# Attention scores on two row halves of the tensor array, two units at a time, with gelu given out in two steps

## The chip, the cores and the metric

The kernel runs on one core of one Trainium2 chip. The metric is the device time of one execution in microseconds (us); the kernel before has three timed runs, 1193.89, 1192.25 and 1193.23 us, and their median is 1193.23 us. The profile is of one further execution, which took 1194.63 us from end to end, of which 1192.8 us are the span that the trace covers.

A core has five engines with a queue of instructions each: TensorE (PE, matrix products; its weight loads are shown apart as PEld), VectorE (DVE), ScalarE (ACT), GpSimd (POOL), and SyncE (SP), which here only starts DMA transfers. Each works its queue in order, and an instruction that has to wait holds up all that stands behind it. SBUF is the memory that the engines work from, PSUM the eight banks that TensorE writes to.

## The reference

Two transformer layers over 512 tokens of width 1024, and 256 context tokens. Layer 0 mixes tokens with a gated product (gelu of an input projection, one half normalised and mixed by a spatial matrix, times the other half) and, beside it, with attention in 8 heads of width 64: a token on the 8 x 64 grid attends to a window of 8 rows and 16 columns, with a position bias, and to all context tokens, under one softmax. Layer 1 is a convolution module. Both have a squared-ReLU MLP. The part that is changed:

```python
    s_loc = jnp.einsum('brqhd,brkwhd->bhrqkw', qg, k_band).astype(jnp.float32) * scale + bias[None]
    s_loc = jnp.where(col_mask[:, None, :], s_loc, NEG)
    s_ctx = jnp.einsum('brqhd,bchd->bhrqc', qg, k_ctx).astype(jnp.float32) * scale
    s = jnp.concatenate([s_loc.reshape(bsz, nh, rows_n, GRID_W, n_loc), s_ctx], axis=-1)
    p = jax.nn.softmax(s, axis=-1).astype(v.dtype)
    out = (jnp.einsum('bhrqkw,brkwhd->brqhd', p_loc, v_band)
           + jnp.einsum('bhrqc,bchd->brqhd', p_ctx, v_ctx))
```

and `jax.nn.gelu(z)` in the gated product. Every layer's six modulation vectors are products of a vector with a matrix, `sc_c @ w_mod[l] + b_mod[l]`.

## The kernel before, in words

A large product is done in three passes of TensorE (`mm3`, L88 to L90): each operand is split into a rounded part "hi" and a rest "lo", and hi x hi, hi x lo and lo x hi are added in one PSUM bank. The split is a CAST (L93) and a subtraction (L94). Weights come as 1 MB tiles (`raw`, L120) in two buffers, are cut into quarters (`W.pieces`, cast on ACT, subtraction on POOL or DVE), and are used from `whi`/`wlo`.

The attention stage lies between about 82 and 236 us of the span. It goes through 16 **units**, 4 pairs of heads (p) times 4 tiles of 128 queries (j). A unit is worked in these steps:

- S, the scores (`scores`, L88 to L90): for each head of the pair 128 queries against 256 windowed keys and 256 context keys into one bank of 128 x 512. Queries, keys and context keys of a pair hold one head on partitions 0 to 63 and the other on 64 to 127. So that a product over all 128 partitions counts one head only, `evac_qk` writes the queries twice, each time with the other head's half multiplied by zero (L542, and L93, L94 for each copy). That gives 12 matmuls of 256 columns for a unit.
- R, on DVE (L771), adds bias and mask and takes the row's minimum of the negated sum; the exponential follows on ACT (L775).
- T, the turn (`turn`, L788): 8 transposes on PE of the unit's probabilities, copied to SBUF by ACT (`pt`, L790). In the last unit of a pair a RECIPROCAL of the row sums stands ahead of it on DVE (L783).
- W, the product with v (`weigh`, L804): 16 matmuls that use 64 columns of the array. After a pair's fourth unit, 8 small matmuls spread the reciprocals (L812, "RECIPbc" below), ACT copies them (`rs`, L816), and DVE scales the pair's output with them (`yb`, L818).

The order is written by hand in the loop over units. Between these steps stands other work: **fills** (`more(1)`, the next step of the generator `filling()`: values of the later pairs, queries and keys of pairs 2 and 3, then the gate with its gelu), mostly 6 matmuls of 512 columns or 12 of 256; and **gemvs** (`work`, L505), the modulation products of later layers, each one DVE pass over 1024 columns of half a 1 MB tile `graw`. There is one buffer for `graw` in this stage, and the load of the next tile (SP, L498) is issued when the second gemv of the tile before is done. 24 gemvs, 12 tiles, fall into this stage, two to a unit. SP's queue also holds the loads of `raw` (each waits until POOL has cut the buffer that it replaces) and of the bias rows (L658). The 12 biases of a pair (`head_bias`, L670) are made on DVE in units j = 2 and j = 3 of the pair ahead.

After the loop the last two row blocks of the gated product are made (`together`, L210 to L213), with a gelu each, and the output projection of the layer begins.

## Time and profile before

| | |
|---|---|
| three timed runs | 1193.89, 1192.25, 1193.23 us, median 1193.23 us |
| profiled execution | 1194.63 us, span 1192.8 us, mean granted TensorE clock 0.993 |
| busy in the span | PE 1162.5 us (97%), DVE 730.5 us (61%), ACT 475.5 us (40%), POOL 173.7 us (15%) |
| attention stage, first scores to first product of `together` | 84.71 to 235.50 us |
| spread of the pairs' reciprocals on PE (L812) | 125.33, 160.45, 199.23 and 231.68 us |

A row of the timeline gives the start in us, the duration, the engine (SPq is SP's queue of DMA issues), the line, the operation, out<-in, the tile's shape on the array (rows\*columns, PE only), the operand's shape and how many are drawn together; in brackets stands how long the engine was idle before and what released it. A row of the stretches gives the stretch, its length, and busy time and count for PE, PEld, DVE, ACT and POOL, then the granted TensorE clock, the busy share of the DMA engines and GB/s. PE's instructions are pipelined, so the time that one takes is read from start to start.

### The profile page before, as it was taken

To read this page: it belongs to the slowest core of one execution; us is meant where nothing else is said; L and a number is where in the kernel's file an instruction comes from. 1 tells how busy PE (TensorE), PEld (TensorE's weight loads), DVE (VectorE), ACT (ScalarE), POOL (GpSimd) and SP (SyncE) were. 2 spreads that over 40 slices of the span, in tenths; PEclk is the share of its full clock that TensorE was granted. 3 is DMA by queue.
4 is the path that set the end of the run, shared out by engine and by line. 5 is a ranking of instruction groups with operands and counts; after the bars stand their busy time and mean duration, and the time that the engine had idled before them with its cause. 6 is when DMAs were issued, how large, how long until landed. Compare 5 with 4: busy or idle time off the path is not lost.

```text
span 1192.8 us, 16638 instructions
## 1 busy us (share of the span) xinstructions
PE 1162.5 (97%) x6662; PEld 968.6 (81%) x6662; DVE 730.5 (61%) x1248; ACT 475.5 (40%) x942; POOL 173.7 (15%) x166
## 2 busy tenths in 40 slices
PE   6999999999999999999999999999999999999997
PEld 2688889779988888888889856688988888888887
DVE  4675777557775666675757778577743443443445
ACT  4463545454632332341425523465642232332423
POOL 1231225263200000000003310044200000000001
PEclk9999999999999999999999999999999999999999
DMA  9624543134155554554543344404132222332322
GB/s 363 233 81 146 186 169 109 70 141 141 60 226 209 182 205 180 207 206 153 208 141 111 108 122 133 130 2 142 36 106 107 84 98 101 105 106 72 106 71 71
DMA packets 30605, 161.91 MB, mean 136 GB/s; under 512 B 4224, under 2 KB 7808, under 8 KB 12608
## 3 DMA queue, kind: packets, MB, share of 16 engines
q1 hardware_dynamic: 30528, 160.85, 38.5%
q8 instruction: 52, 0.85, 0.3%
q14 instruction: 25, 0.20, 0.0%
HBM read 152.52 MB, written 2.10 MB: 130 GB/s over the span
## 4 chain that ended last, share of the span: by engine, by line
PE 80%; DVE 6%; DMA 3%; ACT 2%; issue 1%; POOL 1%; DVEq 0%; SPq 0%; ACTq 0%; POOLq 0%
PE ps L88 21%; PE ps L89 21%; PE ps L90 21%; PE ps L1160 3%; PE ps L213 3%; PE ps L210 3%; PE ps L211 3%; DMA graw<-in_wmB_dram 2%; DVE graw L505 1%; DMA raw<-in_w_ff_dram 1%; PE ps L695 1%; PE ps L804 1%; PE ps L696 1%; PE ps L697 1%; ACT s L775 1%
## 5 line engine op out<-in xcount | busy, mean ns | idle before, releaser
L93 ACT CAST whi<-raw 128x512 fp32r<-128x512 f32 x340 | 191.4, 616 | 198.2 <-PE ps L90 152.6
L88 PE MATMUL ps<-hhi,whi 128*128 128x512 f32 x640 | 253.1, 395 | 1.4 <-ACT hhi L341 1.4
L89 PE MATMUL ps<-hhi,wlo 128*128 128x512 f32 x640 | 250.3, 391 | 1.0 <-DVE wlo L94 1.0
L90 PE MATMUL ps<-hlo,whi 128*128 128x512 f32 x640 | 249.8, 390 | 0.7 <-DVE hlo L349 0.7
L94 DVE TENSOR_TENSOR wlo<-raw,whi 128x512 fp32r<-128x512 f32 x280 | 193.7, 728 | 34.8 <-ACT whi L93 34.0
L90 PE MATMUL ps<-hid,whi 128*128 128x512 f32 (+1 forms) x520 | 196.3, 378 | 0.0
L89 PE MATMUL ps<-hid,wlo 128*128 128x512 f32 (+1 forms) x520 | 196.3, 378 | 0.0
L88 PE MATMUL ps<-hid,whi 128*128 128x512 f32 (+1 forms) x520 | 196.3, 378 | 0.0
L910 DVE SCALAR_TENSOR_TENSOR x<-ps,mod,x 128x512 f32<-128x512 f32 (+1 forms) x94 | 62.7, 668 | 156.5 <-PE ps L90 151.3
L94 POOL TENSOR_TENSOR wlo<-raw,whi 128x512 fp32r<-128x512 f32 x60 | 86.1, 1449 | 478.1 <-ACT whi L93 477.6
L88 PEld LDWEIGHTS ps<-hhi,whi 128*128 128x128 f32 x640 | 120.7, 189 | 33.1 <-issue 6.1
L90 PEld LDWEIGHTS ps<-hlo,whi 128*128 128x128 f32 x640 | 120.6, 188 | 26.6 <-DVE hlo L349 1.0
L89 PEld LDWEIGHTS ps<-hhi,wlo 128*128 128x128 f32 x640 | 120.8, 189 | 25.0 <-DVE wlo L94 1.3
L505 DVE CUSTOM_DVE_ANT_0 graw<-graw,cB,vec 128x1024 f32<-128x1024 f32 x80 | 103.4, 1302 | 18.1 <-DMA graw<-in_wmB_dram 18.1
L88 PEld LDWEIGHTS ps<-hid,whi 128*128 128x128 f32 x520 | 97.8, 188 | 18.2
L90 PEld LDWEIGHTS ps<-hid,whi 128*128 128x128 f32 x520 | 97.8, 188 | 18.2
L89 PEld LDWEIGHTS ps<-hid,wlo 128*128 128x128 f32 x520 | 97.8, 188 | 18.0
L1036 DVE TENSOR_TENSOR z<-z 128x512 f32<-128x512 f32 (+1 forms) x72 | 46.3, 649 | 94.4 <-ACT z L1034 94.4
L1034 ACT ACTIVATE z<-ps 128x512 f32<-128x512 f32 (+1 forms) x72 | 38.9, 550 | 139.4 <-PE ps L90 136.8
L1040 DVE TENSOR_TENSOR hid<-z,hid 128x512 fp32r<-128x512 f32 (+1 forms) x72 | 45.7, 641 | 43.3 <-ACT hid L1038 43.3
L1038 ACT CAST hid<-z 128x512 fp32r<-128x512 f32 (+1 forms) x72 | 40.6, 572 | 51.7 <-DVE z L1036 51.7
L1390 POOL TENSOR_TENSOR o<-o,rstd 128x256 f32<-128x256 f32 x2 | 1.9, 949 | 322.2 <-DVE rstd L322 322.2
(261 smaller groups left out, 1757.2 us busy)
## 6 DMA issues: line engine op xcount, KB each, us to landing
raw<-in_w_ff_dram SPq DMA_DIRECT2D x64, 1024.0 KB
graw<-in_wmB_dram SPq DMA_DIRECT2D x40, 1024.0 KB
raw<-in_w_pw_dram SPq DMA_DIRECT2D x12, 1024.0 KB
raw<-in_w_in_dram SPq DMA_DIRECT2D x10, 1024.0 KB
wmA<-in_wmA_dram SPq DMA_DIRECT2D x7, 1024.0 KB
y<-ypad SPq DMA_DIRECT2D x90, 67.5 KB
raw<-in_w_out_dram SPq DMA_DIRECT2D x4, 1024.0 KB
x<-in_xT_dram SPq DMA_DIRECT2D x8, 256.0 KB
```

The source lines that it names most:

```text
L88: pe.matmul(ps, w[0], a[0], start=first, stop=False)
L89: pe.matmul(ps, w[1], a[0], start=False, stop=False)
L90: pe.matmul(ps, w[0], a[1], start=False, stop=last)
L93: (e or act.copy)(hi, src)
L94: (el or dve).tensor_tensor(lo, src, hi.bitcast(F32), op=ALU.subtract)
L210: pe.matmul(ps, w[0][:, k, c : c + P], a[0], start=n == 0, stop=False)
L505: dve.tensor_tensor_reduce(out=wv, in0=wv, in1=cB, scale=1.0, scalar=vcol(V_BMOD, l * 48 + q * 8 + j % 8), op0=ALU.mult, op1=ALU.add, accu ...
L910: dve.scalar_tensor_tensor(x[:, m, t0:t1], ps, gate[:, m : m + 1], x[:, m, t0:t1], op0=ALU.mult, op1=ALU.add)
L1034: act.activation(z, ps, AF.Relu)
L1036: dve.tensor_tensor(z, z, z, op=ALU.mult)
L1038: act.copy(hi, z)
L1040: dve.tensor_tensor(lo, z, hi.bitcast(F32), op=ALU.subtract)
```

## The change

Lines of the changed program are named by the changed program's numbers; R is L799, the exponential L803, the scores L786, T L816, W L832, RECIPbc L840, yb L846, the reciprocal L811 in it.

- **Scores.** Queries are written once for both heads of a pair, scaled by 0.125 (one ACTIVATE, one CAST, one subtraction where there were two each). Context keys go into the same tile behind the pair's keys. A product takes one head's 64 partitions, on rows 0 to 63 or 64 to 127 of the array, against 512 columns (256 window keys and 256 context keys in one access pattern). A unit has 6 matmuls of 512 columns, the two heads' in turn, where it had 12 of 256 columns.
- **Two units per turn of the loop.** Both units' scores stand together, behind them the products with v of the two units before, then R of the first unit, a fill, R of the second, two or three fills, T of the first, biases of two heads (j = 2), a fill, four gemvs, T of the second, two or three fills. `scores` gives R back as a function. Loads of bias rows are issued two at a time.
- **Gelu in two steps.** `gelu2` yields ahead of its Tanh; the second half is given out at the next fill (`stage`), so another's first half can stand between. The last two gelus start together.
- **Buffers.** The `mblk` pool has 8 tiles where it had 14, `sg` and every second unit's `pt` come from other pools, and the keys have a pool of their own. `graw` keeps its one buffer.

```diff
@@ -532,22 +532,21 @@
     def tok(t):
         return t.rearrange("p (r b c) -> p r b c", b=8, r=8)
 
-    q_s, k_s, kc_s, v_s = {}, {}, {}, {}
+    q_s, k_s, v_s = {}, {}, {}
 
     def evac_qk(m, ps, t0, t1):
         kind, p_ = m
         if kind == "q":
-            for e in range(2):
-                t = slot(s="qt")
-                act.activation(perm(t), tok(ps), AF.Copy, scale=kon[:, C_HEAD + e : C_HEAD + e + 1])
-                pr = (aslot(F32R, "qh"), aslot(F32R, "ql"))
-                split(pr[0], pr[1], t, dve.tensor_copy)
-                q_s[2 * p_ + e] = pr
+            t = slot(s="qt")
+            act.activation(perm(t), tok(ps), AF.Copy, scale=0.125)
+            pr = (aslot(F32R, "qh"), aslot(F32R, "ql"))
+            split(pr[0], pr[1], t, dve.tensor_copy)
+            q_s[p_] = pr
         else:
             t = slot(s="kt")
             act.copy(perm(t), tok(ps))
-            pr = (mslot(F32R, "kh"), mslot(F32R, "kl"))
-            split(pr[0], pr[1], t, dve.tensor_copy)
+            pr = tuple(mp.tile([P, T + TC], F32R, tag="keys", name=nm(n), bufs=4) for n in ("kh", "kl"))
+            split(pr[0][:, :T], pr[1][:, :T], t, dve.tensor_copy)
             k_s[p_] = pr
 
     def first_v():
@@ -582,10 +581,9 @@
             mm3(ps, (w[0][:, k, c : c + P], w[1][:, k, c : c + P]), hc[k], k == 0, k == KC - 1)
             if k == 3:
                 yield
-        t = mslot(F32R, "kc")
-        act.copy(t[:, :TC], ps)
-        dve.tensor_tensor(t[:, TC:], ps, t[:, :TC].bitcast(F32), op=ALU.subtract)
-        kc_s[p_] = (t[:, :TC], t[:, TC:])
+        hi, lo = (t[:, T:] for t in k_s[p_])
+        act.copy(hi, ps)
+        dve.tensor_tensor(lo, ps, hi.bitcast(F32), op=ALU.subtract)
         yield
 
     def turn_v(m, t):
@@ -683,8 +681,21 @@
         t = slot(cols=n, s="gelu")
         act.activation(t, ps, AF.Square, scale=math.sqrt(0.044715))
         dve.scalar_tensor_tensor(t, t, 1.0, ps, op0=ALU.add, op1=ALU.mult)
+        yield
         act.activation(t, t, AF.Tanh, scale=math.sqrt(2.0 / math.pi))
         dve.scalar_tensor_tensor(dst, t, 1.0, ps, op0=ALU.add, op1=ALU.mult)
+
+    staged = deque()
+
+    def stage(n=None):
+
+        for g in list(staged)[:n]:
+            if next(g, 1):
+                staged.remove(g)
+
+    def begin(g):
+        next(g)
+        staged.append(g)
 
     def gate(i):
         w = W.use()
@@ -700,13 +711,18 @@
             if i == 0:
                 gn[n] = mslot(s="gn")
             gt = gn[n][:, i * 256 : (i + 1) * 256]
-            gelu2(gt, ps, 256)
-            for e in range(2):
-                bs = small(6, "bs")
-                dve.bn_stats(bs, gt[:, e * P : (e + 1) * P])
-                dve.bn_aggr(gmv[:, n, 2 * i + e, :], bs)
+
+            def rest(gt=gt, ps=ps, n=n):
+                yield from gelu2(gt, ps, 256)
+                for e in range(2):
+                    bs = small(6, "bs")
+                    dve.bn_stats(bs, gt[:, e * P : (e + 1) * P])
+                    dve.bn_aggr(gmv[:, n, 2 * i + e, :], bs)
+
+            begin(rest())
             yield
         W.free()
+        stage()
 
     def gate_norm(i):
         sd = small(8, "gsd")
@@ -749,19 +768,28 @@
     sm, pts, po, yb, tot = {}, {}, {}, {}, {}
 
     def scores(u):
+
         p_, j = units[u]
         b0 = KSTART[j] // 8
         if j == 0:
             tot[p_] = mp.tile([P, 8], F32, tag="tot", name=nm("tot"), bufs=2)
-        kk = tuple(k_s[p_][i][:, b0 * 64 : b0 * 64 + 256] for i in range(2))
-        pss = []
-        for e in range(2):
-            hd = 2 * p_ + e
-            ps = bank()
-            qh = tuple(q_s[hd][i][:, j * P : (j + 1) * P] for i in range(2))
-            mm3(ps[:, :256], qh, kk, True, True)
-            mm3(ps[:, 256:], qh, kc_s[p_], True, True)
-            pss.append(ps)
+
+        def keys(i, e):
+
+            t = k_s[p_][i][64 * e : 64 * e + 64, :]
+            return bass.AP(t.tensor, t.offset + b0 * 64, [t.ap[0], [T - b0 * 64, 2], [1, 256]])
+
+
+        pss = [bank() for e in range(2)]
+        for n, (a, b) in enumerate(((0, 0), (0, 1), (1, 0))):
+            for e in range(2):
+                pe.matmul(pss[e].rearrange("p (a b) -> p a b", b=256),
+                          q_s[p_][a][64 * e : 64 * e + 64, j * P : (j + 1) * P], keys(b, e),
+                          start=n == 0, stop=n == 2)
+        return lambda: soften(u, pss)
+
+    def soften(u, pss):
+        p_, j = units[u]
         res = []
         for e in range(2):
             hd = 2 * p_ + e
@@ -786,7 +814,7 @@
             pt = bank()
             for i in range(4):
                 pe.transpose(pt[:, i * P : (i + 1) * P], s[:, i * P : (i + 1) * P], ident)
-            t = mp.tile([P, 512], F32, tag="pt", name=nm("pt"), bufs=2)
+            t = blk(s="pt") if u % 2 else mp.tile([P, 512], F32, tag="pt", name=nm("pt"), bufs=2)
             act.copy(t, pt)
             pts[u].append(t)
         del sm[u]
@@ -848,34 +876,38 @@
 
     def more(n):
         for _ in range(n):
+            begun = len(staged)
             if next(fill, 1) is None:
                 nfill[0] += 1
+            stage(begun)
             W.pieces(1, pool)
 
+
     NU = len(units)
-    for u in range(NU):
+    for u in range(0, NU, 2):
         p_, j = units[u]
-        if p_ < 3 and j in (0, 1):
-            rows[2 * p_ + 2 + j] = load_bias(2 * p_ + 2 + j)
-        scores(u)
-        more(1)
+        if p_ < 3 and j == 0:
+            for e in range(2):
+                rows[2 * p_ + 2 + e] = load_bias(2 * p_ + 2 + e)
+        left = [scores(u), scores(u + 1)]
         if u >= 2:
             weigh(u - 2)
+            weigh(u - 1)
+        left[0]()
         more(1)
-        p_, j = units[u]
-        if u >= 1:
-            turn(u - 1)
-        if p_ < 3 and j in (2, 3):
-            head_bias(2 * p_ + j, rows.pop(2 * p_ + j))
+        left[1]()
+        more(2 if u < 8 else 3)
+        turn(u)
+        if p_ < 3 and j == 2:
+            for e in range(2):
+                head_bias(2 * p_ + 2 + e, rows.pop(2 * p_ + 2 + e))
         more(1)
-        work(1 if u in (10, 11) else 2 if u < 13 else 0)
-        if u in (7, 11):
+        work(4 if u < 12 else 0)
+        turn(u + 1)
+        more(2 if u < 8 else 3)
+        if u in (6, 10):
             later.popleft()()
-        if u >= 8:
-            more(1)
     weigh(NU - 2)
-    turn(NU - 1)
-    more(2)
     weigh(NU - 1)
     more(100)
 
@@ -892,12 +924,13 @@
     ev = iter(evs)
     next(ev)()
     W.pieces(1, pool)
+    next(ev)()
+    stage()
+    W.pieces(1, pool)
     operand(2)
     W.pieces(1, pool)
-    next(ev)()
-    W.pieces(1, pool)
     operand(3)
-    
+
     mix.close()
     ma.close()
     xp = ctx.enter_context(tc.tile_pool(name="stream", bufs=1))
```

On DVE, in the first units, the gemvs stand so before (units 0 to 3; `graw` with another number is another 1 MB tile):

```order
L771 ISA st_828 128x1
L505 ISA graw_803,mod_414<-graw_803,cB,vec 128x1024
L505 ISA mod_414 128x1
L505 ISA graw_803,mod_414<-graw_803,cB,vec 128x1024
L505 ISA mod_414 128x1
L771 ISA s_877,st_878<-ps_863,biases 128x512
L771 ISA st_878 128x1
L771 ISA s_881,st_882<-ps_870,biases 128x512
L771 ISA st_882 128x1
L505 ISA graw_858,mod_414<-graw_858,cB,vec 128x1024
```

and so with the change:

```order
L799 ISA s_835,st_836<-ps_807,biases 128x512
L799 ISA st_836 128x1
L505 ISA graw_789,mod_414<-graw_789,cB,vec 128x1024
L505 ISA mod_414 128x1
L505 ISA graw_789,mod_414<-graw_789,cB,vec 128x1024
L505 ISA mod_414 128x1
L505 ISA graw_879,mod_414<-graw_879,cB,vec 128x1024
L505 ISA mod_414 128x1
L505 ISA graw_879,mod_414<-graw_879,cB,vec 128x1024
L505 ISA mod_414 128x1
L799 ISA s_945,st_946<-ps_912,biases 128x512
```

The rows of two tiles now follow one another with no R between them, and the second tile's load can be issued only after the first tile's second row.

At the end of the first pair of heads, DVE before (the reciprocal, then a whole unit's gemvs and R, then the scaling `yb`):

```order
L783 RECIPROCAL tot_808<-tot_808 128x8
L505 ISA graw_1097,mod_415<-graw_1097,cB,vec 128x1024
L505 ISA mod_415 128x1
L505 ISA graw_1097,mod_415<-graw_1097,cB,vec 128x1024
L505 ISA mod_415 128x1
L771 ISA s_1196,st_1197<-ps_1182,biases 128x512
L771 ISA st_1197 128x1
L771 ISA s_1200,st_1201<-ps_1189,biases 128x512
L771 ISA st_1201 128x1
```

and with the change:

```order
L505 ISA graw_1029,mod_414<-graw_1029,cB,vec 128x1024
L505 ISA mod_414 128x1
L505 ISA graw_1029,mod_414<-graw_1029,cB,vec 128x1024
L505 ISA mod_414 128x1
L811 RECIPROCAL tot_797<-tot_797 128x8
L846 TENSOR_TENSOR yb_1126<-ps_928,rs_1124 128x512
L799 ISA s_1128,st_1129<-ps_1083,biases 128x512
L799 ISA st_1129 128x1
```

The reciprocal stands behind the run of four gemvs, and `yb` directly behind the reciprocal, ahead of the next R.

On PE, one unit's scores before, all on the full array:

```order
L88 MATMUL ps_1006<-kh_554,qh_542 128x256
L89 MATMUL ps_1006<-kh_554,ql_543 128x256
L90 MATMUL ps_1006<-kl_555,qh_542 128x256
L88 MATMUL ps_1006<-kc_678,qh_542 128x256
L89 MATMUL ps_1006<-kc_678,ql_543 128x256
L90 MATMUL ps_1006<-kc_678,qh_542 128x256
L88 MATMUL ps_1013<-kh_554,qh_548 128x256
```

and with the change, the two heads' banks in turn, with the products with v (L832) behind two units' scores:

```order
L786 MATMUL ps_920<-kh_548,qh_542 128x512
L786 MATMUL ps_921<-kh_548,qh_542 128x512
L786 MATMUL ps_920<-kl_549,qh_542 128x512
L786 MATMUL ps_921<-kl_549,qh_542 128x512
L786 MATMUL ps_920<-kh_548,ql_543 128x512
L786 MATMUL ps_921<-kh_548,ql_543 128x512
L832 MATMUL ps_928<-pt_860,vtok_765 64x128
```

Six rows for a unit stand where twelve stood, each twice as wide.

## The prediction

> **What bounds the kernel now.** I read the page first, then the stretches of the attention stage, then the timeline of one unit, and last the queues of DVE and SP between two units.

> ```profile
> PE 1162.5 (97%) x6662; PEld 968.6 (81%) x6662; DVE 730.5 (61%) x1248; ACT 475.5 (40%) x942; POOL 173.7 (15%) x166
> PE 80%; DVE 6%; DMA 3%; ACT 2%; issue 1%; POOL 1%; DVEq 0%; SPq 0%; ACTq 0%; POOLq 0%
> 100.00:120.00 20.00, 20.00 (x167) 17.71 (x166) 13.15 (x35) 6.11 (x16) 0.00 (x0) 1.00 0.36 125
> ```

> PE is the bound, over the span (97%) and in the stage (20.00 of 20.00 us), while DVE has a third of its time free (13.15 of 20). So PE work taken out here is time won, as long as DVE's free third stays usable. One unit on PE:

> ```profile
> 113.81 0.28 PE L88 MATMUL ps<-kh,qh 128*128 128x256 f32 x1
> 115.25 0.40 PE L88 MATMUL ps<-hhi,whi 128*128 128x512 f32 x1
> 115.48 0.40 PE L89 MATMUL ps<-hhi,wlo 128*128 128x512 f32 x1
> 116.73 0.66 PE L804 MATMUL ps<-pt,vtok 128*64 128x128 f32 x8
> 117.75 0.50 PE L88 MATMUL ps<-hhi,whi 128*128 128x512 f32 x1
> 118.09 0.40 PE L89 MATMUL ps<-hhi,wlo 128*128 128x512 f32 x1
> 119.25 1.03 PE L788 MATMUL ps<-kon,s 128*128 128x128 f32 x8
> 120.04 0.48 PE L88 MATMUL ps<-hhi,whi 128*128 128x512 f32 x1
> ```

> S takes 115.25 - 113.81 = 1.44, W 1.02, T 0.79; 512 columns take 0.23 from start to start, a fill of six 1.41. Going into W costs about 0.09 and the first product behind it 0.34 instead of 0.23: 0.2 to 0.24 for each change between full array and halves. Now DVE and SP in units 2 and 3:

> ```profile
> 93.98 0.33 SPq L120 DMA_DIRECT2D raw<-in_w_in_dram  x1
> 94.41 0.38 SPq L498 DMA_DIRECT2D graw<-in_wmB_dram  x1
> 101.53 1.29 DVE L505 CUSTOM_DVE_ANT_0 graw<-graw,cB,vec 128x1024 f32<-128x1024 f32 x1 [7.40 <-DMA graw<-in_wmB_dram]
> 102.74 1.28 DVE L505 CUSTOM_DVE_ANT_0 graw<-graw,cB,vec 128x1024 f32<-128x1024 f32 x1
> 103.95 0.69 DVE L771 CUSTOM_DVE_ANT_1 s<-ps,biases 128x512 f32<-128x512 f32 x1
> 104.06 0.33 SPq L498 DMA_DIRECT2D graw<-in_wmB_dram  x1
> 104.56 0.69 DVE L771 CUSTOM_DVE_ANT_1 s<-ps,biases 128x512 f32<-128x512 f32 x1
> 108.94 1.28 DVE L505 CUSTOM_DVE_ANT_0 graw<-graw,cB,vec 128x1024 f32<-128x1024 f32 x1 [2.48 <-DMA graw<-in_wmB_dram]
> ```

> A gemv is 1.21, R 0.61 a head. From a load's issue to its first gemv pass 4.9 us (104.06 to 108.94), or 7.1 with a raw load just ahead of it in SP's queue (94.41 to 101.53). DVE stands still for part of that, but PE has its queue full and doesn't notice.

> **What the change takes from PE.** Six matmuls of 512 columns in pairs of row halves: if two halves overlap fully, 3 x 0.23 = 0.70 a unit, saving 0.74; if not at all, 6 x 0.23 = 1.39, saving 0.05. Nearest row, two other shapes of product:

> ```profile
> 14.19 1.07 PE L392 MATMUL ps<-graw,sc 128*32 128x512 f32 x8 [0.32 <-DMA graw<-in_wmA_dram]
> 18.85 1.02 PE L381 MATMUL ps<-dgc,ones 128*128 128x512 f32 x2
> ```

> Eight quarter-array products of 512 columns took as long as two whole ones, so parts of the array do run side by side; I take 0.70. Sixteen units: 11.8. Scores next to W share its mode change: about 1.0 for all. [...] No run here shows row halves.) Nearly all of the 12.8 is cover that DVE uses up, as follows.

> **What it adds: a load's wait inside DVE's queue.** Two units' four gemvs now stand in a row with one `graw` buffer. The second tile's load is issued behind the first tile's second gemv, so the run is 2.42 + 4.9 + 2.42 = 9.8 us, 5 of them idle, and behind it wait the next R (then the exponential and T on PE) and, at the end of a pair, the reciprocal for which PE's RECIPbc waits. PE can't run ahead: it works its queue in order. The marks for the sum are the four RECIPbc:

> ```profile
> 125.33 1.04 PE L812 MATMUL ps<-kon,tot 128*64 128x128 f32 x16
> 160.45 1.09 PE L812 MATMUL ps<-kon,tot 128*64 128x128 f32 x16 [0.68 <-DVE tot L783]
> 199.23 1.04 PE L812 MATMUL ps<-kon,tot 128*64 128x128 f32 x16
> 231.68 1.04 PE L812 MATMUL ps<-kon,tot 128*64 128x128 f32 x16
> 233.39 0.69 DVE L818 TENSOR_TENSOR yb<-ps,rs 128x512 f32<-128x512 f32 x1 [7.20 <-ACT rs L816]
> 235.50 0.39 PE L210 MATMUL ps<-hhi,whi 128*128 128x512 f32 x1
> ```

> The fills between marks differ, so each stretch of before is corrected by the fills that change sides. (Plus: gained.)

> A, start to first mark. Before it was 125.33 with four more fills ahead, equal to 119.7. After:

> ```profile
> 84.71 0.58 PE L88 MATMUL ps<-kh,qh 128*128 128x256 f32 x1 [2.90 <-DVE kc L587]
> 84.00:86.00 2.00, 1.29 (x6) 1.29 (x7) 0.99 (x4) 0.00 (x0) 0.00 (x0) 0.65 0.92 377
> 86.00:88.00 2.00, 2.00 (x10) 1.90 (x10) 1.02 (x3) 0.76 (x2) 0.00 (x0) 0.50 0.58 219
> 89.28 1.28 DVE L505 CUSTOM_DVE_ANT_0 graw<-graw,cB,vec 128x1024 f32<-128x1024 f32 x1 [0.90 <-DMA graw<-in_wmB_dram]
> 105.17 1.30 DVE L670 TENSOR_TENSOR biases<-rows,kon 128x128 f32<-128x128 f32 x6
> ```

> Two pairs' queries are split here, so two casts and subtractions less (2.2) and the copies ahead of them on ACT shorten DVE's queue at the start by about 3, which removes the 2.90 stall and most of what the clock cost behind it (0.65 and 0.50 in the next two stretches, about 1.5). PE then starts at 81.8. But this is given back at once: tile 0 lands at 89.28 as before, since its load stands in SP's queue behind a raw load that waits for POOL, whose work there is unchanged. From there: 2.42, the second load 6 (between 4.9 and 7.1, a raw load is near), 2.42, four R 2.46, twelve biases 2.46, 2.42, 4.9, 2.42: the reciprocal at about 115. PE alone would be there near 111.5, which is 81.8 plus six S 4.2, four T and four W 7.6, twelve fills 16.9 and mode changes 1.0. **+4.6** (3.5 to 5.7).

> B, first to second mark. Before 35.1, corrected by a fill 33.7. After, on DVE:

> ```profile
> 129.93 1.24 ACT L542 ACTIVATE qt<-ps,kon 128x512 f32<-128x512 f32 x2
> 130.63 0.43 DVE L93 CAST qh<-qt 128x512 fp32r<-128x512 f32 x1 [1.55 <-ACT qt L542]
> 131.09 0.69 DVE L94 TENSOR_TENSOR ql<-qt,qh 128x512 fp32r<-128x512 f32 x1
> ```

> RECIPbc, copy and yb 2.35 (231.68 to 234.0), R 2.46, then the queries' split, whose PE product ends only four fills and a T later: wait 4.3, split 1.1 (0.43 and 0.69, once now where the first row's two copies made it twice); run 9.8; R 2.46; keys' split after 1.6 of waiting, 1.07; biases 2.46, context keys 0.4; run 9.8, reciprocal 0.1; sum 38.0. PE's own work is 29.5, so PE waits, about 8 us, some of it at half clock, which delays the queries by about 1; a raw load beside a graw load 1.5, POOL's accesses beside the biases 1: up to 41.6. I take the middle, 39.8: **-6.1** (-4.3 to -7.9).

> PE's 29.5 is the sum of what stands between the marks: four S 2.8, four W and four T 7.6, twelve fills and seven transposes of v 17.6, RECIPbc 1.0, mode changes 0.5.

> C, second to third. Before 38.8, with the same fills. After, on DVE: 2.35, R 2.46, queries 1.07 (their product is done in time here), run 9.8, keys 1.5, R 2.46, then 8.3 for the two gate products whose half gelus stand in DVE's queue ahead of the next run (48 matmuls of 256 columns at 0.12 is 5.7, and 2.6 for their passes), biases 2.46, run 9.8, 0.1: 40.3. In both runs a raw load stands ahead of the second tile's in SP's queue, 2.2 each by the difference of 7.1 and 4.9, and biases beside POOL 0.5: up to 45.2. I take 42, since before only some raw loads collided: **-3.2** (-1.5 to -6.4).

> D, third mark to `together`. No gemvs in it. Before 199.23 to 235.50, 36.3 from the third mark, and 43.3 with the five fills that move here (7.05); in it were a stall and its clock:

> ```profile
> 211.89 6.08 DVE L718 TENSOR_SCALAR gn<-gn,gmv,gsd 128x128 f32<-128x128 f32 x8 [1.78 <-POOL gsd L714]
> 223.84 1.21 PE L804 MATMUL ps<-pt,vtok 128*64 128x128 f32 x7 [2.04 <-ACT pt L790]
> 224.00:226.00 2.00, 1.95 (x16) 1.42 (x15) 1.97 (x5) 0.27 (x1) 0.00 (x0) 0.64 0.00 0
> 226.00:228.00 2.00, 2.00 (x10) 1.95 (x10) 0.19 (x2) 0.58 (x1) 0.00 (x0) 0.51 0.00 0
> ```

> PE alone would now need 37.9. The last R stands behind the eight `gn` rows (6.08), so T of unit 15 waits 2.3 to 4.2, and the half clock behind such a wait costs (1 - 0.64) x 2 + (1 - 0.51) x 2 = 1.7, once for it and once for the wait at the third mark: 37.9 + 3.4 + 2.3 or 4.2, so 43.6 to 45.5, bounds 39.5 (one slow clock and no stall) to 46. I take 43.9, at the lower of the two: **-0.6** (+3.8 to -2.7). [...]

> E, behind `together`: the two gelus interleave and the wait for the first `yhi` goes:

> ```profile
> 256.95 0.51 PE L210 MATMUL ps<-yhi,whi 128*128 128x512 f32 x1 [0.88 <-ACT yhi L93]
> ```

> **+1.0** (0 to 1). Buffers, and the gelu split inside the fills, I cost at nothing: the second half of a gelu comes one fill later, while PE has the next fill to do, and a PSUM bank of eight is held 1.41 longer; without that cover PE would wait 1.41 for a bank, eight times at most, in C and D, where it waits for DVE anyway. The one ACTIVATE less a pair lies on ACT, which is 40% busy.

> **How the numbers follow.** Sum: 4.6 - 6.1 - 3.2 - 0.6 + 1.0 = -4.3, so the profiled execution goes from 1194.63 to about 1198.9; the median of the runs is 1.4 lower, so **1197.5**. Bounds of all terms: best +5 (1188), worst -12 (1205).

> **Rivals.** (1) DVE's waits stay covered, PE sets the end: 11.8 + 1.0 + start 3.9 (2.90 and 1.0 of the slow clock behind it) + tail 3.6 (2.04 and 1.6 of its clock) + 1.0 = 21, 1172. For it: two-unit turns give PE longer cover, and DVE is 61% busy. Against: DVE's chain in B must then be 29.5 and not 38, with loads that land within 0.7 us of their issue; they took 4.9. Chance 0.07. (2) The chain at its lower ends, loads at 4.9 throughout and no slow clock: 1188 to 1190. Chance 0.13. (3) In between, within 0.2% (2.4 us, about what a measurement of this kernel can tell from no change): the chain lengths of B and C 3 to 4 us shorter than taken, since PE's waits let loads run alone. Chance 0.20. (4) Row halves don't overlap, so the change doesn't do what it says: S 1.39; the 0.69 a unit is hidden where PE waits anyway, not in units 14 and 15: 1.4 more, 1199. It decides only if DVE's chain is shorter than PE's 29.5 + 2.8. Chance 0.08. My forecast, slower by DVE's runs: 0.52.

> Faster 0.07 + 0.13 = 0.20, same 0.20, slower 0.52 + 0.08 = 0.60. The range 1187 to 1205 leaves out rival 1 and the worst ends; the forecast alone spans 1195.6 to 1205.

> **What would show it.** The profile after should have a DVE gemv with 4 to 5 us of idle time behind its DMA in the middle of every run, RECIPbc on PE with waits of 3 to 9 us for `tot` at the first three marks, PE below 80% between the marks, and a granted clock of 0.5 behind them. Starts of S rows two by two with the same start would confirm 0.70. I am wrong if RECIPbc waits less than 1 us, or if the load lands within 3 us because the raw loads no longer run beside it.

## The result

The changed kernel takes 1207.82 us (median of four runs, 1205.54 to 1210.33); the kernel before took 1193.56 (median of its four, 1192.25 to 1196.25). The ratio is 1.0117, with a 95% interval of 1.009 to 1.0144: slower by about 14 us, where 4 were forecast (1197.5, range 1187 to 1205). The direction was right and so was the place, DVE's queue; the size was not, and the time lies outside the range. The profiled execution took 1205.54 us with a span of 1203.8, which is 11.0 more than before. Among all the executions below, two were far slower than the others, one of the kernel before (1943.88) and one with the run at the end of the turn (2535.43), and medians and ratios leave them out.

The page of the changed kernel, and as its last line the same row of `graw` from the page of the kernel before:

```profile
PE 1154.9 (96%) x6566; PEld 959.6 (80%) x6566; DVE 716.3 (60%) x1240; ACT 472.8 (39%) x938; POOL 171.3 (14%) x166
PE 81%; DVE 8%; DMA 5%; ACT 3%; POOL 2%; issue 1%; SPq 0%; DVEq 0%; ACTq 0%; POOLq 0%
L505 DVE CUSTOM_DVE_ANT_0 graw<-graw,cB,vec 128x1024 f32<-128x1024 f32 x80 | 104.3, 1314 | 33.6 <-DMA graw<-in_wmB_dram 33.6
L505 DVE CUSTOM_DVE_ANT_0 graw<-graw,cB,vec 128x1024 f32<-128x1024 f32 x80 | 103.4, 1302 | 18.1 <-DMA graw<-in_wmB_dram 18.1
```

PE is busy 7.6 us less than before (1162.5), though some of that busy time runs at half clock (0.50 in the stretches from 140 to 142 and from 204 to 206 below), and DVE 14.2 less, yet the span is longer. The chain of work that ended last names DMA for 5% (3% before) and DVE for 8% (6%). In the `graw` rows the number behind the last bar is the time that DVE stood idle ahead of a gemv, waiting for a load: 33.6 us, where it was 18.1 before. The scores do what the change says (timeline of PE, units 0 and 1):

```profile
83.26 0.50 PE L786 MATMUL ps<-kh,qh 64*128 64x512 f32 x2
83.60 0.39 PE L786 MATMUL ps<-kl,qh 64*128 64x512 f32 x2
83.83 0.39 PE L786 MATMUL ps<-kh,ql 64*128 64x512 f32 x2
84.85 0.50 PE L88 MATMUL ps<-hhi,whi 128*128 128x512 f32 x1
```

Two matmuls (x2) take 0.23 together, and two units 1.59 from the first score to the next fill: 0.70 a unit and 0.2 for the change from halves to the full array. Where PE stands still after that (same view; the bracket is PE's idle time and what ended it):

```profile
115.69 1.09 PE L840 MATMUL ps<-kon,tot 128*64 128x128 f32 x16 [3.13 <-DVE tot L811]
138.80 1.97 PE L816 MATMUL ps<-kon,s 128*128 128x128 f32 x8 [3.94 <-ACT s L803]
156.45 1.98 PE L840 MATMUL ps<-kon,tot 128*64 128x128 f32 x16 [4.45 <-DVE tot L811]
202.24 0.79 PE L786 MATMUL ps<-kh,qh 64*128 64x512 f32 x1 [10.30 <-DVE gn L686]
206.77 1.04 PE L840 MATMUL ps<-kon,tot 128*64 128x128 f32 x16
234.37 1.36 PE L816 MATMUL ps<-kon,s 128*128 128x128 f32 x8 [2.62 <-ACT s L803]
240.63 1.04 PE L840 MATMUL ps<-kon,tot 128*64 128x128 f32 x16
247.19 0.39 PE L210 MATMUL ps<-hhi,whi 128*128 128x512 f32 x1
```

The four L840 rows are the marks of the prediction. The waits for `tot` at the first two are the forecast ones, and so is that at 138.80, where T waits for the exponential behind R. At the third mark, where a wait for `tot` was forecast too, there is none. The largest wait, 10.30, was not forecast: there a score product of unit 13 waits for `gn`, the second half of a gate's gelu, which is the last reader of the PSUM bank that this product is to write. DVE in those microseconds:

```profile
185.70 4.09 DVE L668 TENSOR_TENSOR biases<-rows,kon 128x128 f32<-128x128 f32 x12
192.15 1.28 DVE L505 CUSTOM_DVE_ANT_0 graw<-graw,cB,vec 128x1024 f32<-128x1024 f32 x1
198.38 1.28 DVE L505 CUSTOM_DVE_ANT_0 graw<-graw,cB,vec 128x1024 f32<-128x1024 f32 x1 [4.94 <-DMA graw<-in_wmB_dram]
200.80 0.20 DVE L811 RECIPROCAL tot<-tot 128x8 f32<-128x8 f32 x1
200.91 0.37 DVE L683 SCALAR_TENSOR_TENSOR gelu<-gelu,ps 128x256 f32<-128x256 f32 x1
201.76 0.42 DVE L686 SCALAR_TENSOR_TENSOR gn<-gelu,ps 128x256 f32<-128x256 f32 x1 [0.48 <-ACT gelu L685]
```

The run of four gemvs, with its 4.94 of waiting for a load in the middle, ends at 200.80. Only then come the reciprocal and the two halves of the gelu, and at 202.18 the bank is free. And what the clock made of the long waits (stretches):

```profile
116.00:118.00 2.00, 2.00 (x21) 1.61 (x17) 0.56 (x1) 0.59 (x1) 0.00 (x0) 1.00 0.82 221
140.00:142.00 2.00, 2.00 (x11) 2.00 (x10) 0.60 (x2) 2.00 (x7) 0.00 (x0) 0.50 0.69 287
204.00:206.00 2.00, 2.00 (x20) 2.00 (x21) 0.00 (x0) 0.00 (x0) 0.00 (x0) 0.50 0.52 217
234.00:236.00 2.00, 1.59 (x10) 1.30 (x11) 0.88 (x4) 2.00 (x7) 0.40 (x1) 1.00 0.00 0
```

Behind 3.94 and 10.30 of idling PE runs at 0.50; behind the 3.13 at 115.69 and the 2.62 at 234.37 the clock stays at 1.00.

### The profile page after: what moved, and what is told of

Read it like the earlier page. It is cut to its first block, busy times and chain, and to the rows that moved or that the text cites. A ratio compares the mean times of both kernels' runs of the same rounds, so it can differ in the third digit from the quotient of the medians.

```text
span 1203.8 us, 16457 instructions
## 1 busy us (share of the span) xinstructions
PE 1154.9 (96%) x6566; PEld 959.6 (80%) x6566; DVE 716.3 (60%) x1240; ACT 472.8 (39%) x938; POOL 171.3 (14%) x166
## 3 DMA queue, kind: packets, MB, share of 16 engines
HBM read 152.52 MB, written 2.10 MB: 128 GB/s over the span
## 4 chain that ended last, share of the span: by engine, by line
PE 81%; DVE 8%; DMA 5%; ACT 3%; POOL 2%; issue 1%; SPq 0%; DVEq 0%; ACTq 0%; POOLq 0%
PE ps L88 21%; PE ps L89 21%; PE ps L90 21%; PE ps L213 3%; PE ps L210 3%; PE ps L211 3%; PE ps L1193 3%; DMA graw<-in_wmB_dram 3%; DVE graw L505 3%; ACT s L803 1%; DMA raw<-in_w_ff_dram 1%; DVE biases L668 1%; DMA wmA<-in_wmA_dram 1%; DVE acc L311 1%; PE ps L392 1%
## 5 line engine op out<-in xcount | busy, mean ns | idle before, releaser
L93 ACT CAST whi<-raw 128x512 fp32r<-128x512 f32 x340 | 191.2, 615 | 198.2 <-PE ps L90 173.2
L88 PE MATMUL ps<-hhi,whi 128*128 128x512 f32 x640 | 254.0, 397 | 1.6 <-ACT hhi L341 1.6
L89 PE MATMUL ps<-hhi,wlo 128*128 128x512 f32 x640 | 251.2, 393 | 1.0 <-DVE wlo L94 1.0
L94 DVE TENSOR_TENSOR wlo<-raw,whi 128x512 fp32r<-128x512 f32 x280 | 193.8, 729 | 34.2 <-ACT whi L93 33.3
L89 PE MATMUL ps<-hid,wlo 128*128 128x512 f32 (+1 forms) x520 | 196.6, 378 | 0.0
L88 PE MATMUL ps<-hid,whi 128*128 128x512 f32 (+1 forms) x520 | 196.5, 378 | 0.0
L94 POOL TENSOR_TENSOR wlo<-raw,whi 128x512 fp32r<-128x512 f32 x60 | 85.3, 1438 | 477.7 <-ACT whi L93 477.6
L88 PEld LDWEIGHTS ps<-hhi,whi 128*128 128x128 f32 x640 | 121.2, 189 | 34.2 <-issue 5.6
L89 PEld LDWEIGHTS ps<-hhi,wlo 128*128 128x128 f32 x640 | 121.3, 190 | 25.5 <-DVE wlo L94 1.3
L505 DVE CUSTOM_DVE_ANT_0 graw<-graw,cB,vec 128x1024 f32<-128x1024 f32 x80 | 104.3, 1314 | 33.6 <-DMA graw<-in_wmB_dram 33.6
L88 PEld LDWEIGHTS ps<-hid,whi 128*128 128x128 f32 x520 | 97.9, 188 | 18.1
L89 PEld LDWEIGHTS ps<-hid,wlo 128*128 128x128 f32 x520 | 97.9, 188 | 18.1
```

Of the source, the lines that this page charges most:

```text
L88: pe.matmul(ps, w[0], a[0], start=first, stop=False)
L89: pe.matmul(ps, w[1], a[0], start=False, stop=False)
L93: (e or act.copy)(hi, src)
L94: (el or dve).tensor_tensor(lo, src, hi.bitcast(F32), op=ALU.subtract)
L505: dve.tensor_tensor_reduce(out=wv, in0=wv, in1=cB, scale=1.0, scalar=vcol(V_BMOD, l * 48 + q * 8 + j % 8), op0=ALU.mult, op1=ALU.add, accu ...
```

## The experiments

Twelve kernels besides the change, in the order in which they ran. All times are medians; the ratio is to the kernel before on the same chip, with its 95% interval.

| kernel | us | ratio |
|---|---|---|
| the change | 1207.82 | 1.0117 [1.009, 1.0144] |
| gemvs spread two and two | 1190.99 | 0.9977 [0.9955, 0.9999] |
| no second load | 1178.80 | 0.9873 [0.9852, 0.9893] |
| scores alone | 1188.46 | 0.9944 [0.9927, 0.9961] |
| run of four alone, in the kernel before | 1213.96 | 1.0163 [1.0146, 1.0179] |
| gelu whole | 1206.37 | 1.0112 [1.0086, 1.0138] |
| run at the end of the turn | 1197.89 | 1.0035 [1.0019, 1.0051] |
| loads in halves | 1198.99 | 1.0048 [1.0029, 1.0067] |
| spread, loads in halves | 1185.86 | 0.9937 [0.9916, 0.9957] |
| one head's scores behind the other's | 1206.83 | one execution |
| scores alone, loads in halves | 1184.27 | 0.9917 [0.9902, 0.9931] |
| products with v ahead of the scores | 1209.60 | 1.0126 [1.0111, 1.0141] |
| spread, halves, three orders mended | 1182.95 | 0.9911 [0.9895, 0.9928] |

### The gemvs spread two and two

```diff
         left[0]()
+        work(2 if u < 12 else 0)
         more(1)
...
-        work(4 if u < 12 else 0)
         turn(u + 1)
+        work(2 if u < 12 else 0)
```

> The change, with the four gemvs of a turn given out as two behind R of the first unit and two behind T of the second, so that R of the second unit stands between two tiles and the reciprocal ahead of the second tile's gemvs. Theory (the run of four gemvs with a load's wait in DVE's queue sets the pace): a load is 4.9 and two gemvs 2.42, twice in a turn 14.6, about PE's 14.75 for a turn, so the waits for tot (7.6 in the change) and the 10.3 ahead of the scores of unit 13 go, the marks come 30 to 33 apart, and the time falls to 1172 to 1185. Rival (the pairing itself holds PSUM banks too long, whatever DVE does): the 10.3 stays, 1195 to 1200. Rival (row halves make it slow): 1203 or more.

Measured 1190.99, 17 less than the change: its whole loss comes back, but the time is 6 above the theory's range. The waits for `tot` are gone; what is left on PE is

```profile
90.97 1.97 PE L816 MATMUL ps<-kon,s 128*128 128x128 f32 x8 [2.26 <-ACT s L803]
138.92 1.97 PE L816 MATMUL ps<-kon,s 128*128 128x128 f32 x8 [3.15 <-ACT s L803]
186.20 0.79 PE L786 MATMUL ps<-kh,qh 64*128 64x512 f32 x1 [3.50 <-DVE gn L686]
218.05 1.36 PE L816 MATMUL ps<-kon,s 128*128 128x128 f32 x8 [2.65 <-ACT s L803]
```

The bank wait at unit 13 shrank from 10.30 to 3.50 with the length of what stands ahead of the gelu on DVE. The rival that the pairing holds banks by itself, whatever DVE does, falls; so does the one that blames the row halves.

### No second load

```diff
-        if i < 40:
+        if i < 12 and i % 2:
+            gemv_tile[i] = last_tile[0]
+        elif i < 40:
...
+            last_tile[0] = t
```

> The change, with the loads of the odd gemv tiles below 12 left out: their gemvs run over the buffer that the tile before left, so the modulation products of those tiles are not computed. Order and number of instructions on DVE are the change's; only the load's wait inside the run of four is gone (a run is 4.8 and not 9.8). Theory (it is the wait): the chain from mark to mark is 2 x 5 shorter, PE-bound again, 1173 to 1186. Rival (the four gemvs' own 4.84 in a row is what R and the reciprocal wait for): no better than 1200. Rival (a bank held by a half gelu that has its second half late): 10.3 stays at unit 13, about 1195.

Measured 1178.80, 29 less than the change, in the theory's range. The kernel leaves out the modulation products of the odd tiles. Order and count on DVE are the change's, so the four gemvs' own 4.84 are not what costs the 29: the marks stand at 111.20, 142.53, 181.56 and 217.64, and PE's waits are 2.04 for `tot`, 2.45 for the bank and 2.64 for R. Half of the stage's gemv traffic is gone too; the loads in halves, further down, test whether that is part of the gain.

### Only the scores

The loop of the kernel before (one unit a turn, gemvs two by two, gelu whole) with the change's `evac_qk`, `ctx_k` and scores; the buffers stay the change's.

> Only the scores on row halves, with queries written once and context keys behind the keys: one unit at a time as before, gelu whole, gemvs two to a unit. Theory: a unit's scores take 0.70 and not 1.44, less 0.2 for one more change between halves and full array, so 16 x 0.54 = 8.6 from PE, and about 3 to 4 at the start where the query splits went: 1178 to 1185. Rival (row halves do not pay beside weight loads, or the DVE work behind them is the bound without pairing): 1191 to 1196.

Measured 1188.46: 6 less than before, 3.5 short of the range's end. PE waits in it 3.16 for `pt` and 0.90 for `yhi`, waits that are there before too (2.04 and 0.88), and 0.87 and 0.47 at places where it didn't wait before. The start is clean, 0 where 2.90 stood. So row halves pay, but less than I had put on them: from the first score to `together` the profiled execution takes 146.5 where it took 150.8 before, 4.3 less, and the slow clock behind the old start (about 1.5, my estimate from the 0.65 and 0.50 of the two stretches behind it) is part of that; 8.6 were forecast for the scores.

### Only the run of four, in the kernel before

```diff
-        work(1 if u in (10, 11) else 2 if u < 13 else 0)
+        work(4 if u % 2 and u < 12 else 0)
```

> The kernel before, with four gemvs in a row behind every second unit in place of two behind each. Theory (the run costs where R or the reciprocal of the next step stands right behind it and PE needs it within some 10 us): before, R of a unit is needed by T only about 14 us later, so most of the run's 9.8 is covered: 1193 to 1199. Rival (a run of four with one buffer costs wherever it stands): 1203 or more.

Measured 1213.96, 19 slower, well outside what I expected: the rival holds. Where the time goes (PE's timeline):

```profile
139.28 0.39 PE L88 MATMUL ps<-kh,qh 128*128 128x256 f32 x1 [1.80 <-DVE st L771]
160.66 0.38 PE L88 MATMUL ps<-kh,qh 128*128 128x256 f32 x1 [2.94 <-DVE st L771]
187.88 1.03 PE L804 MATMUL ps<-pt,vtok 128*64 128x128 f32 x7 [1.27 <-ACT pt L790]
210.19 0.58 PE L88 MATMUL ps<-kh,qh 128*128 128x256 f32 x1 [4.43 <-DVE gn L687]
```

T needs R late enough, as I had argued. But R is also what frees the score's PSUM bank, and a gelu frees the gate's: in three of the four rows PE's next scores wait for a bank that a reader behind the run still holds. In the third (187.88) the product with v waits for a copy of `pt` that stands in ACT's queue behind an exponential, and that one had waited for R behind the run:

```profile
183.61 0.73 ACT L775 ACTIVATE s<-s,st 128x512 f32<-128x512 f32 x1 [8.74 <-DVE st L771]
```

The run alone is +1.63%, the scores alone -0.56%, together +1.06%, and the change measures +1.17%. The sum agrees within the intervals, but the waits behind it do not: PE's longest wait is 4.43 here and 10.30 in the change, so that the agreement may be luck in part. Nor does it show that two units a turn cost nothing by themselves; for that the spread version (0.9977) stands beside the scores alone (0.9944), and their intervals just overlap.

### Gelu whole

```diff
-        yield
+        yield from ()
...
-        next(g)
-        staged.append(g)
+        if next(g, 1) is None:
+            staged.append(g)
```

> The change with gelu given out whole, as before. Theory (what stands behind the run in DVE's order waits for it, both halves alike): the first half of the third gate's gelu is already behind the run, so the bank that PE waits for is not free earlier: 10.3 at unit 13 stays within 1 us; the 0.9 behind the last products comes back: 1206 to 1210. Rival (the second half given out late holds the bank): the 10.3 shrinks by at least 4, 1198 to 1203.

Measured 1206.37, and the wait at unit 13 is 11.74, which is 1.4 more and not within the 1 that I gave it; giving out the second half late isn't what holds the bank. Both halves stand behind the run. The 0.9 that I expected back behind the last products did not come.

### The run at the end of the turn

```diff
-        work(4 if u < 12 else 0)
         turn(u + 1)
         more(2 if u < 8 else 3)
+        work(4 if u < 12 else 0)
```

> The change with the four gemvs at the end of the turn, behind T of the second unit and its fills, nothing else moved. The run is as long as in the change and has the same load's wait. Theory (what counts is what stands next behind the run): the reciprocal and the gate's gelus are ahead of the run now, so the waits for tot and the 10.3 for a bank go; behind it stand R of the next two units, which T needs some 8 us after their scores, while the run reaches some 7 into that: 1178 to 1190. Rival (a run of four with its wait costs DVE time wherever it stands): 1203 to 1210.

Measured 1197.89, 10 better than the change, 8 short of the theory. The waits for `tot` and for the bank are gone, as expected; in their place T waits for R, which now stands behind the run:

```profile
135.97 1.97 PE L816 MATMUL ps<-kon,s 128*128 128x128 f32 x8 [5.09 <-ACT s L803]
176.19 1.97 PE L816 MATMUL ps<-kon,s 128*128 128x128 f32 x8 [3.22 <-ACT s L803]
201.67 1.62 PE L816 MATMUL ps<-kon,s 128*128 128x128 f32 x8 [3.77 <-ACT s L803]
```

Neither of the two places hides the run of 9.8; the place decides who waits, and for how long.

### Loads in halves

```diff
-        if e:
+        if i < 11:
+            t = gemv_tile[i]
+            gemv_tile[i + 1] = t
+            sync.dma_start(t[:, e * D : (e + 1) * D], I["wmB"][i + 1][:, e * D : (e + 1) * D])
+            gpool[1] = max(gpool[1], i + 2)
+        elif e:
```

> The change with each gemv tile loaded in two halves of 512 KB into the same one buffer: half e of the next tile is loaded as soon as gemv e of this tile is done. The wait in the run is then the load of a half less one gemv, 1.3 to 3.7 by a load of 2.5 to 4.9, in place of 5. Theory (the time follows the wait: leaving the second loads out took 5 from each of six runs and 29 from the time): 6 x 1.3 to 3.7 less, 1186 to 1200. Rival (what the run without loads gained came from less traffic on the DMA engines): 1203 or more.

Measured 1198.99, 8.8 less than the change, inside the range. The waits within the six runs add up to 31.0 in the change (5.34, 5.04, 4.91, 4.98, 5.83, 4.94) and to 24.2 here (4.66, 4.46 and 4.78 in the three runs that have a raw load issued 1.1 to 1.8 us ahead of the first half's, 3.1 to 3.6 in the others). So 6.8 less waiting brought 8.8, and in the kernel without second loads 31.0 less brought 29.0: the time follows the wait by 1.3 and 0.9 to one. Here the same bytes are moved (the page has 152.52 MB read from HBM here and in the change, 146.23 without second loads), so the rival that put the gain down to less traffic falls.

### Spread, with loads in halves

The edits of the spread version and of the loads in halves together.

> The change with the gemvs spread two and two and loads in halves. Theory: what was left in the spread version are waits of T for R behind a gemv pair's load (2.26, 3.15, 1.08) and 3.5 for a bank, each with slow clock; with the half loaded 1.2 to 3.6 earlier most of these go: 1177 to 1186, below the scores alone (1188). Rival (those waits are not loads): 1188 to 1192.

Measured 1185.86, at the upper end of the theory's range. PE still waits 1.93, 2.24 and 2.65 for R and 2.73 for the bank at unit 13. Of the waits that were to go, not each had slow clock behind it: in the spread version products of 512 columns start 0.43 and 0.42 apart behind the 2.26 and the 3.15 (93.16 to 93.59, 141.12 to 141.54), and the scores left of unit 13 take 1.58 behind the 3.50 (186.20 to 187.78; 0.89 in the mended kernel, 179.59 to 180.48), but behind the 1.08 products start 0.23 apart (159.74 to 160.65).

### One head's scores behind the other's

```diff
-        for n, (a, b) in enumerate(((0, 0), (0, 1), (1, 0))):
-            for e in range(2):
+        for e in range(2):
+            for n, (a, b) in enumerate(((0, 0), (0, 1), (1, 0))):
```

> The change with one head's three score products given out before the other head's three, the array halves the same. Read is the price of a unit's scores from the starts on PE: 0.70 in the change with the heads in turn. Theory (two halves run side by side only where neighbours in PE's queue are on different halves): 6 x 0.23 = 1.39 less one overlap where the heads meet, so 1.1 to 1.4 a unit; the time within 0.5% of the change, since PE waits for DVE there. Rival (PE looks further ahead than the next instruction): 0.7 to 0.8.

My theory was wrong, the rival right. The program gives out three products on rows 0 to 63 and then three on 64 to 127, and they run side by side all the same, two starts together (timeline of PE, unit 2 and the first row behind unit 3):

```profile
94.06 0.50 PE L786 MATMUL ps<-kh,qh 64*128 64x512 f32 x2
94.39 0.40 PE L786 MATMUL ps<-kl,qh 64*128 64x512 f32 x2
94.63 0.40 PE L786 MATMUL ps<-kh,ql 64*128 64x512 f32 x2
95.64 0.66 PE L832 MATMUL ps<-pt,vtok 128*64 128x128 f32 x8
```

The 12 products of the two units take 1.58, as in the change (1.59). The time, 1206.83 in one execution, is the change's.

### Scores alone, with loads in halves

> Scores alone on row halves (one unit at a time, gelu whole, two gemvs a unit) with the gemv tiles loaded in halves. Theory (a load's wait on DVE costs only where PE then waits): in that version PE waits 3.2, 0.9, 0.9 and 0.5, none of them for R behind a gemv, so the earlier loads gain nothing: 1186 to 1190, within 0.2% of 1188.5. Rival (DVE's waits are paid everywhere): 1183 or less.

Measured 1184.27, between what the theory and what the rival expected, against 1188.46 for scores alone, whose runs were beside other runs of the kernel before; the intervals of the two ratios overlap. The profiled spans are 1184.0 and 1184.4. PE's two longer waits are the same (3.16 and 0.89), but the 0.87 and 0.47 of the scores alone are gone, and from the first score to `together` it takes 143.5 where the scores alone take 146.5; its first score came 2.4 later, which hides this in the span. With one trace of each, whether the earlier loads gain up to 4 us here or nothing stays open.

### Products with v ahead of the scores

```diff
-        left = [scores(u), scores(u + 1)]
         if u >= 2:
             weigh(u - 2)
             weigh(u - 1)
+        left = [scores(u), scores(u + 1)]
```

> The change with the two due products with v and RECIPbc ahead of the two units' scores in place of behind them. Theory (at unit 13 PE stands before a score product whose bank the third gate's gelu holds, and that is behind the run on DVE; W and RECIPbc, which need 4.5 more after it, then come behind the wait): with W ahead they are done in the wait, and the third mark comes right after the reciprocal, C 3 to 5 shorter. But at the other marks the scores now wait behind the reciprocal and R with them, 1.5 each: 1201 to 1208 in all. Rival (C was long for DVE's chain alone, the bank wait costs nothing of its own): C as in the change, 50, and 1209 to 1213.

Between the second and the third mark the theory holds: 45.0 (159.25 to 204.28) where the change has 50.3 (156.45 to 206.77), and PE waits at the third mark for the reciprocal instead of for the bank:

```profile
159.25 1.12 PE L840 MATMUL ps<-kon,tot 128*64 128x128 f32 x8 [9.11 <-DVE tot L811]
204.28 1.97 PE L840 MATMUL ps<-kon,tot 128*64 128x128 f32 x16 [7.75 <-DVE tot L811]
```

So the mark comes 0.35 behind the reciprocal, where it comes 5.97 behind it in the change, with DVE's chain as long (45.0 and 44.7 from reciprocal to reciprocal). Not all of the 5.3 is won, for the scores of two units have moved behind the mark: from the reciprocal to the first fill behind these scores it is 4.6 (203.93 to 208.53) and in the change 6.9 (200.80 to 207.74), 2.3 less. In all it is 1209.60, the change's time within the noise, more than I expected and in the rival's range. At the second mark scores and R now wait behind RECIPbc too (43.7 from the first mark, 40.8 in the change). Behind the third, `together` comes after 47.2 (40.4): the scores stand there, and T's wait for R in the last turn is 3.66, with products of 512 columns 0.43 apart behind it (238.39 to 240.10), where behind the change's 2.62 they are 0.23 apart (235.80 to 236.72).

### Three orders mended

Spread and halves, and in the first turn both pairs of gemvs behind R of both units, in the sixth the second pair behind the gate's gelu, in the last R of unit 15 ahead of the fill with the `gn` rows.

```diff
-        work(2 if u < 12 else 0)
+        work(2 if 0 < u < 12 else 0)
+        if u == 14:
+            left[1]()
         more(1)
-        left[1]()
+        if u < 14:
+            left[1]()
+        work(2 if u == 0 else 0)
...
-        work(2 if u < 12 else 0)
+        work(2 if u < 10 else 0)
         more(2 if u < 8 else 3)
+        work(2 if u == 10 else 0)
```

> The spread version with loads in halves, and three orders mended: the first turn's gemvs behind R of both units, the sixth turn's second pair behind the gate's gelu, and in the last turn R of unit 15 ahead of the fill with the eight gn rows. Theory (each wait left there is one of these, and each brings some 1.6 of slow clock): 1.93, 2.73 and 2.65 go with 2 to 4.8 of clock, 1175 to 1181. Rival (the waits move on to the next instruction): 1183 to 1186.

Measured 1182.95 (1180.33 to 1185.45), 0.9911 of the kernel before and the fastest complete kernel here, though its lead on the scores alone with halves (1184.27) is inside the noise. Half of the theory, half of the rival (and of the three waits that were each to bring slow clock, the 2.65 brought none: in the kernel with the gemvs spread and loads in halves products of 512 columns start 0.23 apart behind it, 217.57 to 218.48): the bank wait fell to 0.84 and T's wait in the last turn is gone, but the 1.93 of the first turn came back as 1.70 in the second, and the spatial products now wait for the `gn` work that R was put ahead of (the last line is a stretch):

```profile
105.41 1.36 PE L821 MATMUL ps<-kon,s 128*128 128x128 f32 x8 [1.70 <-ACT s L808]
136.90 1.36 PE L821 MATMUL ps<-kon,s 128*128 128x128 f32 x8 [2.04 <-ACT s L808]
212.71 2.05 PE L748 MATMUL ps<-wsp,gn 128*128 128x128 f32 x16 [3.22 <-DVE sg L751]
212.00:214.00 2.00, 1.29 (x11) 1.29 (x12) 2.00 (x5) 0.00 (x0) 0.00 (x0) 1.00 0.86 279
```

## Why the prediction was wrong, and where it was right

The terms by the marks of the profiled executions (before, corrected by the fills that change sides as in the prediction, less after):

| term | forecast | measured |
|---|---|---|
| A, start to first mark | +4.6 | 119.7 - 115.7 = +4.0 |
| B, first to second | -6.1 | 33.7 - 40.8 = -7.1 |
| C, second to third | -3.2 | 38.8 - 50.3 = -11.5 |
| D, third to `together` | -0.6 | 43.3 - 40.4 = +2.9 |
| E, behind it | +1.0 | +0.9, the wait is gone |
| sum | -4.3 | -10.8 (spans: -11.0) |

**What held.** That a load's wait inside DVE's queue takes all that the row halves give, and more. The run's wait was forecast at 4.9 (4.91 to 5.83 measured), the first reciprocal at 115 (115.35), B at 39.8 (40.8) with about 8 of waiting in it (3.94 and 4.45), a unit's scores at 0.70. The kernel without second loads and the one with halves show that it is the wait; the spread version, that it is the place in the queue. Of the signs that I had named, the half clock came behind the 3.94 and the 4.45 (0.50 from 140 to 142 and from 158 to 160) and not behind the 3.13 at the first mark (1.00 from 116 to 118). Rival 4, row halves that don't overlap, falls by the starts. Rival 1, 1172 with PE as the bound, is approached only when the waits are gone (1178.80).

**The step that failed is term C, and in it the wait for a PSUM bank, which I had put at nothing.** C came out 8.3 worse than forecast and below its own lower end (-6.4); the whole sum is short by 6.5, since D gave 3.5 back. Two things are in the 8.3. DVE's chain from reciprocal to reciprocal was 44.7 (156.10 to 200.80) where I took 42, so 2.7 longer, but inside my upper end of 45.2: the biases took 4.09 for 2.46 (POOL was busy beside them, from 183.76 to 187.62; before, six biases took 3.48 beside POOL, at 147.09, and 1.30 without it, at 105.17), and one run waited 5.83 for its load. And the mark came 5.97 behind the reciprocal, where it was 0.35 at the second mark, so 5.6 more: PE wasn't waiting at RECIPbc but one step earlier, at a score product of unit 13, so that scores, sixteen products of each W and the half clock (0.50 from 204 to 206) came behind the wait instead of being covered by it. The sentence at fault is "Buffers, and the gelu split inside the fills, I cost at nothing ... a PSUM bank of eight is held 1.41 longer". I had looked for what the gelu split does to a bank, which is nothing that shows (gelu whole: 1206.37), and not for what the run does to every bank whose reader stands behind it. The kernel with the products with v ahead of the scores shows it: with the same run and the same chain on DVE the mark is back at 0.35 behind the reciprocal, and C is 5.3 shorter, though part of that is work moved behind the mark. The run alone in the kernel before shows it again, and there I made the same mistake a second time: I followed T's need for R and left out that R frees a bank.

**D** was too dark: the wait of T came as forecast (2.62, between 2.3 and 4.2), but its half clock did not, and the wait at the third mark had moved into C. There my reading of one row, 2.04 of idling and then 0.64 and 0.51, did not carry over: behind the 2.62 the clock was 1.00 (stretches from 234 to 236 and 236 to 238). See below.

**The rest of the miss** is in the comparison: the profiled execution of the change (1205.54) was its fastest, 2.3 under its median, while before's lay 1.1 above its median. I carried a difference between single executions over to medians and shifted it by 1.4 the other way. The upper end of the range was also added up wrong: the worst ends of the five terms, 3.5 - 7.9 - 6.4 - 2.7 + 0, make -13.5 and not -12, which is 1206.7. The measured 1207.82 lies outside that as well.

## What to carry to other kernels

When work is grouped on an engine that takes its queue in order, as DVE does in these traces (the change's third reciprocal starts at 200.80, behind the run, though the last exponential of its pair ended at 182.9), count the longest stretch that can now stand in its queue, transfers' waits included, and then list everything behind it twice: who needs its output, and who needs the buffer that it frees. A group of passes over one buffer contains its own load's wait (4.91 to 5.83 here); with other work between the passes part of it is covered (at most 4.07 is left in the spread version), and less stands behind it. A saving on the bounding engine is worth what the next engine's queue lets through: here the matmul change (-0.56%) and the regrouping (+1.63%) were measured apart, and their sum comes near the whole (+1.17%).

## What the runs showed of the hardware

The clock's drop behind a wait of 2 to 3 us is not a fixed price. Before, 2.04 of idling was followed by 0.64 and 0.51 (stretches from 224 to 226 and 226 to 228). In the changed kernel 2.62 and 3.13, and in the mended one 1.70, 2.04 and 3.22, were followed by 1.00 (stretches from 106 to 108, from 136 to 138 and from 212 to 214), while 3.94 and 10.30 were followed by 0.50. Even the same wait, that of T for R in the last turn, goes either way: behind 2.62 in the change and 2.65 in the spread version products of 512 columns start 0.23 apart (235.80 to 236.72 and 219.49 to 220.40), behind 2.64 in the kernel without second loads and 2.62 with loads in halves 0.43 apart (211.95 to 213.23 and 229.12 to 230.40). The length of a wait alone does not tell which it will be; what does, these runs do not show.
